# One step of a token mixer: side pieces ahead of the additions of landed rows, or behind them

## The chip, the cores and the metric

The kernel runs on one core of a Trainium2 chip. A core has five engines with instruction queues of their own: TensorE (PE in the profile, its weight loads PEld), VectorE (DVE), ScalarE (ACT), GpSimd (POOL) and SyncE (SP), which here issues nearly all DMAs. The metric is the device time of one execution in microseconds (us); less is better.

## The reference, cut to what matters

One transformer layer on 256 tokens of width 2048, all in float32: a first SwiGLU block, a token mixer, a second SwiGLU block. Ahead of each block the input is normalised, scaled and shifted by rows that a vector `c` yields through one large matrix `w_ada` (2048 x 18432); its nine parts are shift, scale and gate of the three blocks.

```python
ada = (jax.nn.silu(c) @ w_ada + b_ada)[:, None, :]
sh1, sc1, g1, sh2, sc2, g2, sh3, sc3, g3 = jnp.split(ada, N_ADA, axis=-1)
h = _swiglu(_modulate(x, sh1, sc1), ffn1_w_in, ffn1_w_out)
x = _layernorm(ALPHA * x + 0.5 * (1 + g1) * h, ln1_g, ln1_b)
h = _token_mixer(_modulate(x, sh2, sc2), w_in, ...)   # 8 softmax heads with forget gates, 4 mLSTM heads
x = _layernorm(ALPHA * x + (1 + g2) * h, ln2_g, ln2_b)
h = _swiglu(_modulate(x, sh3, sc3), ffn2_w_in, ffn2_w_out)
x = _layernorm(ALPHA * x + 0.5 * (1 + g3) * h, ln3_g, ln3_b)
```

## The kernel before, in words

**Large products.** Each float32 factor is split into a rounded part `hi` and a rest `lo`, and a product is three matmuls (`mm3`, L391 to L393). Weights come in loads of 1 MB (`load_w`, DMA issued by SP at L374) into three buffers `raw`; ACT casts them to `hi` (L145), DVE subtracts to get `lo` (L146), 1024 columns at a time, into six buffers of each kind.

**The ada rows.** `silu(c) @ w_ada` has one row on the left, so it isn't run on PE: for each of 16 blocks of 128 rows, a piece of 512 KB of `w_ada` (tile `ar`, three buffers under the tag `araw`, issued by SP at L168) is scaled by a column of `silu(c)` and added to a tile `acc` on DVE (`ada_acc`, L158 for the first piece, L160 for the others). When 16 pieces are in, a few small steps ("columns") end the group: for a gate, ACT and DVE split `acc` into two tiles that also take `araw` buffers, PE sums over the partitions into two PSUM tiles `bc` (L180), and DVE adds them to `gate` (L217); for a pair of shift and scale, PE transposes (`at`, L193) and DVE reduces (L196). This work is spread over the whole kernel by `pump(n)`: it first adds what was issued in an earlier call (`add_landed`), then runs one small step of a group that is ending (`end_columns`), then issues new pieces, some `n` per call and never more than two that have not been added.

**The mixer.** Its projections run as units of 1 MB of weights, and after each unit `step()` (L991) is called: 4 times in each of four projections of `cols_form_b`, 4 times in each of six of `form_a_pair`, and 12 times in the first two passes of the output projection, 52 in all. `step()` calls `pump(R_MX)` and `advance(NP)`. `advance` takes up to two pieces of the heads' work from the list `side`, each a generator: gates, convolutions, mLSTM heads (`mlstm_head`, `mlstm_out` with its transposes `ytp`, L1244), softmax heads (`fox_head`: logits `lps` on PE, L1078; masks, maxima and reciprocals on DVE, L1083 to L1087; exponentials on ACT, L1086; transposes `ptp`, L1093). The list is empty for the first eight steps; `gates()` is put on it after them. The side pieces issue no DMA. Small PSUM tiles (`aux_tile`: `bc`, `at`, `lps`, `ptp`, `ytp` and so on) share three banks.

**What sets the order.** The program as traced in Python gives each instruction its rank; a planner then fixes each engine's queue from its own estimates of durations: of the instructions that it takes for ready it queues the one of the lowest rank. So rank decides only among ready instructions. One thing binds harder: `ada_acc` calls `tc.keep_in_program_order`, which queues the addition behind the DVE instruction that was traced just ahead of it. On the chip each queue is then fixed, with semaphores where one engine needs another. A DMA that waits for a buffer holds up what stands behind it in SP's queue.

Of the kernel before, what the change touches and what calls it, by code (L numbers as in the profile page):

```python
# [47 lines left out]
def layer_kernel(  # L48
# [178 lines left out]
    def add_landed():  # L227
        while landing:
            ada_acc(*landing.pop(0))

    def end_columns():
        if ada["ends"] and next(ada["ends"], 0) == 0:
            ada["ends"] = None
            ada["done"] += 1

    def next_row():
        if not ada["rows"]:
            if not ada["left"]:
                return ENDED
            ada["rows"] = ada["left"].pop(0)  # L240
        got = next(ada["rows"])
        if got in (None, PAUSE):
            return got
        ada.update(ends=got, rows=None, beside=0)
        next(got)
        return STARTED

    def pump(n):
        add_landed()
        end_columns()  # L250
        ada["owed"] = min(ada["owed"] + n, 3)
        while ada["owed"] >= 1 and len(landing) < 2 and not (ada["ends"] and ada["beside"]):
            got = next_row()
            if got == ENDED:
                break
            if got != STARTED:
                ada["owed"] -= 1
                ada["beside"] += 1
            if got == PAUSE:
                break  # L260
# [427 lines left out]
    NP = 2  # L688
# [288 lines left out]
    def advance(n):  # L977
        for g in list(side):
            if n == 0:
                break  # L980
            got = next(g, 0)
            if got == 0:
                side.remove(g)
            n -= got is not True
# [4 lines left out]
            advance(NP)  # L989

    def step():  # L991
        pump(R_MX)
        advance(NP)

    def wait(names):
        while not done.issuperset(names):
# [3 lines left out]
    def cols_form_b(c0, col, ws, use, name):  # L1000
        ps = {(a, b): mm_tile(f"b_{name}{col}{a}{b}") for b in range(len(ws)) for a in range(2)}
        cb = [sum(ws[:b]) for b in range(len(ws) + 1)]
        copies = emptied[-1:]
        for u in range(4):
            for k4, hi, lo in load_w(W[u * 512:(u + 1) * 512, c0 + col:c0 + col + cb[-1]], 4, cb[-1],
                                     f"{name}{col}_{u}", copies=copies if u else ()):
                k = u * 4 + k4
                for a in range(2):
                    ts_ = slice(a * P, (a + 1) * P)
                    for b in range(len(ws)):  # L1010
                        bs = slice(cb[b], cb[b + 1])
                        mm3(ps[a, b][:, :ws[b]], xhi[:, k, ts_], xlo[:, k, ts_], hi[:, bs], lo[:, bs],
                            k == 0, k == KD - 1)
            step()
        for b in range(len(ws)):
            for a in range(2):
                use(col + cb[b], a, ps[a, b], ws[b])
# [19 lines left out]
    def form_a_pair(ca, cb, name):  # L1037
        ps = [mm_tile(f"pr_{name}{i}") for i in range(2)]
        copies = emptied[-1:]
        cols_form_a(W, ca, [p[:, :T] for p in ps], xT, f"{name}a", step, copies=copies)  # L1040
        cols_form_a(W, cb, [p[:, T:] for p in ps], xT, f"{name}b", step)
        return ps
# [438 lines left out]
```

## Time and profile before

| what | value |
|---|---|
| median of 3 runs | 1930.63 us (1930.4 to 1932.44) |
| the profiled execution, its own time | 1933.45 us |
| its span, first to last instruction | 1931.8 us |
| PE busy / weight loads busy | 97% / 89% of the span |
| DVE busy / ACT busy | 76% / 48% |
| DMA | 510.89 MB, mean 264 GB/s |
| granted TensorE clock | 0.998 of full |

The profile is that of one execution, so sums are made against its 1933.45 us. Busy times are unions of an engine's instructions. A number behind a row's `x` is a count; "[0.77 <-DVE gate L217]" says that the engine sat idle for 0.77 us ahead of that instruction, and what ended it. The stretch in which `side` has work and `step()` is called runs from about 880 to 1130 us.

### The profile page before, as it was taken

To read this page: it belongs to the slowest core of one execution; us is meant where nothing else is said; L and a number is where in the kernel's file an instruction comes from. 1 tells how busy PE (TensorE), PEld (TensorE's weight loads), DVE (VectorE), ACT (ScalarE), POOL (GpSimd) and SP (SyncE) were. 2 spreads that over 40 slices of the span, in tenths; PEclk is the share of its full clock that TensorE was granted. 3 is DMA by queue.
4 is the path that set the end of the run, shared out by engine and by line. 5 is a ranking of instruction groups with operands and counts; after the bars stand their busy time and mean duration, and the time that the engine had idled before them with its cause. 6 is when DMAs were issued, how large, how long until landed. Compare 5 with 4: busy or idle time off the path is not lost.

```text
span 1931.8 us, 32165 instructions
## 1 busy us (share of the span) xinstructions
PE 1882.0 (97%) x13109; PEld 1726.2 (89%) x13109; DVE 1466.0 (76%) x1774; ACT 931.4 (48%) x1296; POOL 54.2 (3%) x85
## 2 busy tenths in 40 slices
PE   3999999999999999999999999999999999999997
PEld 3999999999988888598999776999999999988886
DVE  7889979877778899678787787777775654555776
ACT  3554354444354464745664544555444444444562
POOL 1211100000000000000000000000000000000000
PEclk9999999999999999999999999999999999999999
DMA  9988969989799887489778784998777656655552
GB/s 354 356 312 304 332 209 315 327 297 335 267 336 315 274 302 259 154 311 318 266 252 288 282 296 147 324 313 270 236 260 257 226 196 197 228 189 193 196 195 89
DMA packets 295819, 510.89 MB, mean 264 GB/s; under 512 B 10834, under 2 KB 158962, under 8 KB 294648
## 3 DMA queue, kind: packets, MB, share of 16 engines
q1 hardware_dynamic: 287896, 480.53, 73.2%
q0 software_dynamic: 7776, 28.32, 4.2%
q8 instruction: 102, 1.67, 0.4%
q14 instruction: 45, 0.37, 0.1%
HBM read 506.71 MB, written 2.10 MB: 263 GB/s over the span
## 4 chain that ended last, share of the span: by engine, by line
PE 90%; DVE 5%; DMA 3%; ACT 1%; issue 1%; POOL 0%; SPq 0%; DVEq 0%; ACTq 0%; POOLq 0%
PE gu_f L391 8%; PE gu_f L393 8%; PE gu_f L392 8%; PE o_f L391 8%; PE o_f L393 8%; PE o_f L392 8%; PE s L391 4%; PE s L392 4%; PE s L393 4%; PE pr_f L393 2%; PE pr_f L392 2%; PE pr_f L391 2%; PE fh L393 2%; PE fh L392 2%; PE fh L391 2%; PE fs L392 1%
## 5 line engine op out<-in xcount | busy, mean ns | idle before, releaser
L160 DVE SCALAR_TENSOR_TENSOR acc<-ar,csil,acc 128x1024 f32<-128x1024 f32 x240 | 306.9, 1279 | 33.0 <-DMA ar<-in_w_ada_dram 32.6
L391 PE MATMUL s<-xhi_f,hi_s 128*128 128x256 f32 x768 | 213.3, 279 | 1.7 <-ACT xhi_f L325 0.9
L392 PE MATMUL s<-xlo_f,hi_s 128*128 128x256 f32 x768 | 213.0, 278 | 0.1
L393 PE MATMUL s<-xhi_f,lo_s 128*128 128x256 f32 x768 | 212.4, 277 | 0.0
L393 PE MATMUL gu_f<-xhi_f,lo_f2i 128*128 128x256 f32 x768 | 212.0, 276 | 0.0
L392 PE MATMUL gu_f<-xlo_f,hi_f2i 128*128 128x256 f32 x768 | 212.0, 276 | 0.0
L391 PE MATMUL gu_f<-xhi_f,hi_f2i 128*128 128x256 f32 x768 | 212.0, 276 | 0.0
L146 DVE TENSOR_TENSOR lo_f2i<-raw_f2i,hi_f2i 128x1024 fp32r<-128x1024 f32 x96 | 117.6, 1225 | 100.1 <-ACT hi_f2i L145 100.0
L391 PE MATMUL gu_f<-xhi_f,hi_f1i 128*128 128x256 f32 x640 | 176.8, 276 | 0.0
L393 PE MATMUL gu_f<-xhi_f,lo_f1i 128*128 128x256 f32 x640 | 176.7, 276 | 0.0
L392 PE MATMUL gu_f<-xlo_f,hi_f1i 128*128 128x256 f32 x640 | 176.7, 276 | 0.0
L145 ACT CAST hi_f2i<-raw_f2i 128x1024 fp32r<-128x1024 f32 x96 | 100.8, 1050 | 137.5 <-PE gu_f L392 125.5
L145 ACT CAST hi_s<-raw_s 128x1024 fp32r<-128x1024 f32 x96 | 100.2, 1053 | 114.0 <-PE s L392 86.8
L391 PEld LDWEIGHTS s<-xhi_f,hi_s 128*128 128x128 f32 x768 | 144.8, 189 | 2.0 <-ACT xhi_f L325 1.1
L392 PEld LDWEIGHTS s<-xlo_f,hi_s 128*128 128x128 f32 x768 | 145.0, 189 | 0.4 <-DVE xlo_f L327 0.3
L393 PEld LDWEIGHTS s<-xhi_f,lo_s 128*128 128x128 f32 x768 | 144.6, 189 | 0.3 <-DVE lo_s L146 0.3
L392 PEld LDWEIGHTS gu_f<-xlo_f,hi_f2i 128*128 128x128 f32 x768 | 144.2, 188 | 0.1
L391 PEld LDWEIGHTS gu_f<-xhi_f,hi_f2i 128*128 128x128 f32 x768 | 144.2, 188 | 0.1
L393 PEld LDWEIGHTS gu_f<-xhi_f,lo_f2i 128*128 128x128 f32 x768 | 144.2, 188 | 0.0
L145 ACT CAST hi_f1i<-raw_f1i 128x1024 fp32r<-128x1024 f32 x80 | 83.6, 1050 | 114.6 <-PE gu_f L392 80.3
L146 DVE TENSOR_TENSOR lo_f2o<-raw_f2o,hi_f2o 128x1024 fp32r<-128x1024 f32 x86 | 105.3, 1224 | 43.2 <-ACT hi_f2o L145 43.1
L145 ACT CAST hh<-hT 128x512 fp32r<-128x512 f32 x126 | 77.3, 620 | 114.1 <-PE o_f L392 113.8
(490 smaller groups left out, 5406.9 us busy)
## 6 DMA issues: line engine op xcount, KB each, us to landing
ar<-in_w_ada_dram SPq DMA_DIRECT2D x240, 512.0 KB, 5.9
raw_s<-in_ffn_w_in_dram SPq DMA_DIRECT2D x48, 1024.0 KB, 7.3
raw_f2i<-in_ffn_w_in_dram SPq DMA_DIRECT2D x48, 1024.0 KB, 5.1
raw_f1o<-in_ffn_w_out_dram SPq DMA_DIRECT2D x44, 1024.0 KB, 7.8
raw_f2o<-in_ffn_w_out_dram SPq DMA_DIRECT2D x44, 1024.0 KB, 5.1
raw_f1i<-in_ffn_w_in_dram SPq DMA_DIRECT2D x40, 1024.0 KB, 7.7
ar<-in_w_ada_dram POOLq DMA_DIRECT2D x48, 512.0 KB, 6.9
raw_mxo<-in_w_out_dram SPq DMA_DIRECT2D x16, 1024.0 KB, 8.1
```

Source lines behind the costliest of these rows:

```text
L145: S.copy(hi, src)
L146: V.tensor_tensor(out=lo, in0=src, in1=hi.bitcast(F32), op=ALU.subtract)
L160: ins = V.scalar_tensor_tensor(out=acc, in0=raw, scalar=csil[:, k:k + 1], in1=acc, op0=ALU.mult, op1=ALU.add)
L391: PE.matmul(o, ah, bh, start=start, stop=False)
L392: PE.matmul(o, ah, bl, start=False, stop=False)
L393: return PE.matmul(o, al, bh, start=False, stop=stop)
```

## The change

In `step()` the two calls change places. Nothing is added or removed.

```diff
     def step():
+        advance(NP)
         pump(R_MX)
-        advance(NP)
```

Ahead of it, the additions of a step were traced behind the last split of the unit's weights, and the side pieces behind them; after it, the additions, the small ending steps and the new `ar` loads of a step are traced behind the side pieces of that step.

## Rows read from the trace of the kernel before

**Rows 1.** The page's first lines: span; busy us (share) x instructions.

```profile
span 1931.8 us, 32165 instructions
PE 1882.0 (97%) x13109; PEld 1726.2 (89%) x13109; DVE 1466.0 (76%) x1774; ACT 931.4 (48%) x1296; POOL 54.2 (3%) x85
```

**Rows 2.** Waits of PE, whole span: us in total, times, longest.

```profile
PE cp L741 <- DVE gate L160: 14.8, 1, 14.8
...
PE ptp L1093 <- ACT s L1088: 1.4, 2, 1.0
...
PE ytp L1244 <- DVE gate L217: 0.8, 1, 0.8
...
PE o_mx L393 <- DVE ylo L146: 0.2, 1, 0.2
```

**Rows 3.** Stretches: us, busy us of PE, PEld, DVE, ACT, POOL; PEclk, DMA share, GB/s.

```profile
1090.00:1130.00 40.00, 38.91 (x181) 31.80 (x180) 29.51 (x38) 19.81 (x35) 0.00 (x0) 1.00 0.94 330
1130.00:1185.00 55.00, 54.74 (x262) 45.16 (x260) 47.22 (x69) 18.30 (x25) 2.88 (x4) 1.00 0.68 229
```

**Rows 4.** Groups of 880 to 1130 us: count, busy us, mean ns, idle before, releaser.

```profile
L160 DVE SCALAR_TENSOR_TENSOR acc<-ar,csil,acc 128x1024 f32<-128x1024 f32 x48 | 61.3, 1278 | 5.4 <-DMA ar<-in_w_ada_dram 5.3
L146 DVE TENSOR_TENSOR lo_fv<-raw_fv,hi_fv 128x1024 fp32r<-128x1024 f32 x8 | 9.6, 1219 | 1.5 <-ACT hi_fv L145 1.5
```

**Rows 5.** Waits of SP's queue in 880 to 1130 us: total, times, longest.

```profile
SPq L168 <- DVE acc L160: 55.1, 35, 3.5
SPq L168 <- DMA ar<-in_w_ada_dram: 22.5, 12, 4.7
```

**Rows 6.** Timeline near 1017 us, all engines: start, us, instruction, [idle before].

```profile
1016.46 0.41 PE L180 MATMUL bc<-alo,trir 128*128 128x512 f32 x1
...
1016.71 0.60 PE L1244 MATMUL ytp<-ident,og 128*128 128x128 f32 x4
1017.34 1.28 DVE L217 SCALAR_TENSOR_TENSOR gate<-bc,gate 128x512 f32<-128x512 f32 x2
...
1018.08 0.66 PE L1244 MATMUL ytp<-ident,og 128*128 128x128 f32 x4 [0.77 <-DVE gate L217]
...
1019.67 0.48 DVE L1251 SCALAR_TENSOR_TENSOR yl<-ytp,hcol,yh 128x256 fp32r<-128x256 f32 x1
```

**Rows 7.** Timeline near 1084 us, all engines.

```profile
1083.64 0.75 DVE L158 TENSOR_SCALAR acc<-ar,csil 128x1024 f32<-128x1024 f32 x1 [1.77 <-DMA ar<-in_w_ada_dram]
...
1084.24 0.82 PE L1078 MATMUL lps<-qs 128*128 128x128 f32 x4
1084.31 1.22 DVE L146 TENSOR_TENSOR lo_mxo<-raw_mxo,hi_mxo 128x1024 fp32r<-128x1024 f32 x1
...
1085.44 0.73 DVE L1083 SCALAR_TENSOR_TENSOR s<-lps,ccol,mask 128x128 f32<-128x128 f32 x2
```

**Rows 8.** Timeline near 1120 us, all engines.

```profile
1118.85 1.28 DVE L160 SCALAR_TENSOR_TENSOR acc<-ar,csil,acc 128x1024 f32<-128x1024 f32 x1
...
1119.66 0.18 ACT L1086 ACTIVATION_READ_ACCUMULATOR s<-s,nm 128x1 f32 x1
1120.05 0.22 DVE L1087 RECIPROCAL nm<-nm 128x1 f32<-128x1 f32 x2
...
1120.69 0.84 PE L1093 MATMUL ptp<-ident,s 128*128 128x128 f32 x3 [1.01 <-ACT s L1088]
```

**Rows 9.** Timelines of DVE and PE near 1038 and 1065 us.

```profile
1037.16 0.17 DVE L1087 RECIPROCAL nm<-nm 128x1 f32<-128x1 f32 x1 [1.01 <-ACT s L1086]
1038.10 2.58 DVE L146 TENSOR_TENSOR lo_f1a<-raw_f1a,hi_f1a 128x1024 fp32r<-128x1024 f32 x2 [0.77 <-ACT hi_f1a L145]
...
1039.52 0.28 PE L393 MATMUL pr_f<-xhi_mx,lo_f1a 128*128 128x256 f32 x1
...
1064.51 2.36 DVE L146 TENSOR_TENSOR lo_fv<-raw_fv,hi_fv 128x1024 fp32r<-128x1024 f32 x2 [1.51 <-ACT hi_fv L145]
...
1066.04 0.40 PE L392 MATMUL b_fv<-lo_fv,xhi_mx 128*128 128x512 f32 x1
```

## Prediction

> **What bounds the kernel now.** I read the page's busy times first, then the waits of PE, then the stretch of the mixer, then the waits of SP's queue, and last the timelines around each wait of PE in the mixer. PE is busy for 97% of the span, DVE for 76% [rows 1]. So PE is the engine to ask about, and its waits say where time could be won. The longest of them, 14.8 us, lies ahead of the first product of the kernel and has nothing to do with the mixer [rows 2]. Between 880 and 1130 us, where the change can act, PE waits in three ways only: 1.4 us in two waits of the transposes `ptp` for ACT's scaled exponentials, 0.8 us in one wait of `ytp` for the addition to `gate`, and 0.2 us for a split of `yF` [rows 2]. Together that is 2.4 us, or 0.12% of the time. None of PE's waits in the mixer is for a DMA or for a split of weights, although SP's queue stands still for 55.1 us in that stretch because an `ar` buffer is not yet added (35 times, up to 3.5 us) and 22.5 us more because its former load has not landed [rows 5]. So PE has weights ahead of it, and what the mixer loses is little.
>
> What a measurement of this kernel can tell from no change is about 0.2%, or 3.9 us. The waits that the change could remove are smaller than that.
>
> [...]
>
> **The change, part by part.** Nothing is added or removed. Three kinds of work are moved behind the side pieces of the same step: the additions (48 of 1278 ns and three shorter first ones between 880 and 1130 us [rows 4]), the small ending steps of a group, and the issue of the `ar` loads. The side pieces issue no DMA, so the order in which SP meets the weight loads and the `ar` loads stays as it was; what changes is when an `ar` buffer is free. In the first eight steps there is no side piece and nothing changes. When the rows' groups end does not matter for the rest: each has steps to spare ahead of its use, and the number of rows per step is the same.
>
> *The ending step of a gate, at 1017 us.* Before, the two `bc` tiles take two of the three small PSUM tiles first, the first `ytp` the third, and the second `ytp` waits 0.77 us for the addition to `gate` [rows 6]. After, the two `ytp` come first, then the first `bc`; the second `bc` waits for the first `ytp` to be read. That reading is two pairs of one ACT and one DVE instruction, of which one DVE takes 0.48 us [rows 6]: with three of such a size in a row, 1.4 us, less what PE does in between (the second `ytp`, 0.66 us, and a matmul of `bc`, 0.25 us from its start to the next), some 0.5 us. The ends are 0 (the planner puts products there) and 1.8 us (one more DVE instruction of 1.28 us [rows 4] ahead of the reading). I take 0.5, the sum of the nearest rows: 0.5 less 0.8 is -0.3 us.
>
> *The logits at 1084 us.* DVE stands 1.77 us for a row that has not landed, adds it, splits weights, and only at 1085.44 masks the logits, which PE ended at 1084.24 + 0.82 = 1085.06 [rows 7]. With the addition behind, the mask can start at most 0.4 us sooner. One of PE's two waits for `ptp` hangs on it, with 1.4 less 1.0, or 0.4 us [rows 2]. Ends: 0 and -0.4; the split of 1.22 us stays in front unless it too moves up, so I take the middle, -0.2 us.
>
> *The reciprocal at 1120 us.* An addition that starts at 1118.85 ends at 1120.13 by its duration, the exponentials it keeps waiting were done at 1119.66 + 0.18 = 1119.84, and the reciprocals go at 1120.05 [rows 8]. Behind it, they would go some 0.2 us sooner. PE's wait there is 1.01 us [rows 8], and most of it is the chain mask, maximum, exponential itself. Ends: 0 and -1.0; I take -0.2 us.
>
> *Additions that now stand behind a side piece and ahead of a tight split.* Near 1038 us the last reciprocal of two heads goes at 1037.16, the split of `f1a` starts at 1038.10 after a wait for ACT and its first half is done 1.22 us later, at 1039.32; PE uses it at 1039.52, with 0.2 us to spare [rows 9, 4]. Near 1065 us the split of `fv` ends at 1064.51 + 1.22 = 1065.73, and PE uses it at 1066.04, with 0.3 us to spare [rows 9, 4]. An addition that is tied to the last reciprocal falls just ahead of such a split. Before 1038.10 there is an idle time of 0.77 us, so one addition of 1.28 us costs 0.5 us of delay, of which 0.2 is covered: +0.3 us. Before 1064.51 there is 1.51 us of idle, which covers one addition. Ends: 0, when no row is due there, and +4.6 us, when two additions (2.56 us) delay each of the two splits in full: 2.56 - 0.2 + 2.56 - 0.3. I take one at the first place, +0.3 us, since a step issues 1.42 rows on the mean.
>
> *Later `ar` loads.* An addition that goes later frees its buffer later, and SP, which waits for it, holds up the weights behind it. Ends: 0, since even 55.1 us of such waits cost PE nothing now, and +3.5 us, one longest wait passed on in full [rows 5]. I take +0.4 us, near the first end, by the row that shows no wait of PE for weights [rows 2].
>
> *Loads that no longer hold DVE.* DVE stood 5.3 us for rows that had not landed [rows 4]. That mostly goes, as rows have longer to land; what is late next is the split for which ACT's cast is awaited, so I count nothing beyond the three waits above.
>
> The sum: 1933.45 - 0.3 - 0.2 - 0.2 + 0.3 + 0.4 = 1933.45 us for the profiled execution. It stands 2.8 us above the median of the runs, 1930.63, and the change is the same there: 1930.6 us.
>
> **The rivals.**
>
> *The planner's queues hardly change.* Rank decides only among ready instructions, and rows that landed early may already stand where the new order puts them; only the tie of `ada_acc` binds. For it: the addition at 1118.85 already stands amid a head's work [rows 8]. Against it: the tie is to the DVE instruction traced last, which is another one now in each step with a side piece that uses DVE. It gives 1930.6 us too. Chance 0.14.
>
> *DVE's late additions reach PE (slower).* The mechanism is that of the tight splits above, with two additions at both: +4.6 us, 1935.2. It decides from the point at which additions behind a last reciprocal exceed the idle time and the 0.2 and 0.3 us to spare [rows 9]. For it: DVE takes its queue in order, and at 1083.64 an addition has already held up a split and a mask for 1.77 us [rows 7]. Against it: the additions would have to bunch at just these places. Chance 0.19.
>
> *All waits of PE in the mixer go.* 1.4 + 0.8 + 0.2 is 2.4 us: 1928.2. For it: in two of the three chains an addition stands [rows 7, 8]. Against it: the chain of a head through ACT remains. Chance 0.09; a quarter of that goes beyond, to more than 3.9 us.
>
> *PE loses more than its waits show.* If a mere fiftieth of the 11% in which no weights are loaded [rows 1] were idle time that the side pieces cause, 0.02 x 210 = 4.2 us would go: 1926.4. [...] Chance 0.06.
>
> **How the numbers follow.** My forecast, that the moves take place and add up to nothing, has 0.52. Faster by more than 3.9 us: 0.06 and a quarter of 0.09, 0.08 in all. Slower by more than 3.9 us: 0.19. Within: the forecast, the first rival and the rest of the third, 0.73. The range reaches down to 1927.0, just past all waits gone, and up to 1936.5, past the slower rival's 1935.2 with a third of the 3.5 us of SP's longest wait added; some 0.08 is left out on each side, a little more above.
>
> **What would show it right or wrong.** Right: PE's waits between 880 and 1130 us stay between 1 and 4 us in total, `ytp` no longer waits for `gate`, a `bc` waits for a DVE or ACT instruction on `ytp` instead or nothing does, and DVE's waits for rows fall well below 5.3 us. The slower rival: PE waits for a `lo_` split, near 1038 or 1065 us above all, with an addition just ahead of it on DVE. SP's queue waiting on additions for much more than 55.1 us, with PE or ACT waiting for a `raw_` load and PE for the split behind it, would show my term for late loads too small. The prediction is wrong if the start of the second block's first product moves by more than 4 us either way, or if time is won or lost outside of 880 to 1130 us.

## The result

The kernel changed takes 1936.19 us (median of 8 runs, 1934.27 to 1938.6), the kernel before 1931.78 us beside it (8 runs); the ratio is 1.0023, 95% interval 1.0014 to 1.0031. A second set of 11 runs gave 1935.73 against 1932.32 us, ratio 1.0018 (1.0010 to 1.0027). One run of all, at 2104.6 us with a granted clock of 0.852 (`e10`, below), was in a slower state and is left out of every median and ratio. The change costs 3.4 to 4.4 us, where I had forecast none. The time lies inside the range of 1927.0 to 1936.5, but the case that came about is the slower one, to which I gave 0.19.

The profile after, with the lines that answer to those of before. First the page's head [rows 1]:

```profile
span 1933.8 us, 32176 instructions
PE 1883.5 (97%) x13109; PEld 1727.7 (89%) x13109; DVE 1468.0 (76%) x1774; ACT 931.3 (48%) x1296; POOL 55.1 (3%) x85
```

The same work is done in a span 2.0 us longer. What PE waits for, whole span [rows 2]:

```profile
PE bc L180 <- DVE gate L217: 2.2, 1, 2.2
...
PE pr_f L393 <- DVE lo_f0a L146: 0.8, 1, 0.8
...
PE ptp L1093 <- ACT s L1088: 0.5, 1, 0.5
PE o_mx L391 <- ACT yhi L145: 0.4, 1, 0.4
...
PE b_fv L392 <- DVE lo_fv L146: 0.2, 1, 0.2
```

`ytp` no longer waits, and one of the two waits for `ptp` is gone; in their place stand `bc` with 2.2, `lo_f0a` with 0.8, `yhi` with 0.4 and `lo_fv` with 0.2 us. With the 0.2 us for `ylo` that stand there as before, PE waits 4.3 us in the mixer, 2.4 before; the 14.8 us ahead of the kernel's first product are as they were. SP's queue from 880 to 1130 us [rows 5]:

```profile
SPq L168 <- DVE acc L160: 108.4, 38, 12.8
```

Its wait for additions doubles, and the longest goes from 3.5 to 12.8 us. The additions themselves, in the groups of that stretch [rows 4], take as long as before and wait 3.3 us for rows instead of 5.3:

```profile
L160 DVE SCALAR_TENSOR_TENSOR acc<-ar,csil,acc 128x1024 f32<-128x1024 f32 x48 | 61.5, 1280 | 3.6 <-DMA ar<-in_w_ada_dram 3.3
```

**Where the time went.** Spans of single executions differ by some us for reasons that have nothing to do with the mixer, so I cut the trace at PE's first matmul on certain tiles: the first `pr_m` product (about 902 us), the first `pr_f` product on `f0a`, on `f1a` and on `f1b`, the first `o_mx` product, its first on `kept`, and the first of the second block (`ge`). Each number is the time from one such start to the next, in us; the first column is the time ahead of `pr_m`.

```
                        to m0a  m0a-f0a  f0a-f1a  f1a-f1b  f1b-o_mx  o_mx-kept  kept-ge   m0a-ge
before                  902.6   101.88    27.22    14.48     39.37     76.26     23.28    282.49
e1_before_again         901.4   101.88    26.59    14.48     39.37     76.35     23.28    281.95
after                   902.2   101.88    29.78    14.59     40.58     74.76     23.27    284.87
e9_after_again          902.2   101.88    29.88    14.62     40.44     74.75     23.27    284.85
e2_ends_first           901.8   101.88    31.10    14.53     40.71     74.75     23.27    286.26
e3_bc_other_bank        905.5   101.88    27.22    15.95     40.64     74.75     23.27    283.72
e4_gate_end_later       901.0   101.88    26.75    17.79     42.25     75.20     23.77    287.64
e5_loads_last           900.9   101.88    26.89    14.59     39.38     75.72     23.28    281.75
e6_adds_first           900.6   101.88    26.33    14.55     39.37     78.56     23.28    283.98
e7_outproj_only         902.3   101.88    26.53    14.48     39.37     75.09     23.28    280.63
e10_outproj_again       903.3   101.88    27.00    14.50     39.37     75.20     23.27    281.24
e8_proj_only            900.4   101.88    29.95    14.48     40.92     74.75     23.28    285.25
e11_free_additions      900.2   105.36    27.97    16.19     39.38     74.63     23.28    286.81
e12_ar_by_pool          905.3   101.88    29.30    14.60     40.14     74.77     23.28    283.96
```

What is ahead of `pr_m` scatters over 5 us without system, most of it in the first block, from PE's first `s` product to its first `gu_f` product (about 38 to 310 us; it takes 270.2 to 274.1); in two executions of one kernel the rest repeats to 0.15 us, but for the stretch from `f0a` to `f1a`, in which `ytp` waits now and then. Mean against mean of two executions each, the kernel changed loses 2.9 us from `f0a` to `f1a`, 0.1 and 1.1 in the next two stretches, and wins 1.6 us from `o_mx` to `kept`: 2.6 us in all. Up to `o_mx` that is 4.2 us, though PE's waits there (2.2, 0.8, 0.4 and 0.2 us) add up to 3.6: here 0.6 us of the loss do not stand in the idle time that the profile shows.

**From f0a to f1a: two additions among the `og` pieces, and the cast of `ahi`.** DVE's timeline of the kernel changed near 1005 us, then ACT's:

```profile
1004.11 1.28 DVE L160 SCALAR_TENSOR_TENSOR acc<-ar,csil,acc 128x1024 f32<-128x1024 f32 x1
1005.30 0.48 DVE L1238 SCALAR_TENSOR_TENSOR og<-yM,rr,og 128x256 f32<-128x256 f32 x1
1005.70 1.28 DVE L160 SCALAR_TENSOR_TENSOR acc<-ar,csil,acc 128x1024 f32<-128x1024 f32 x1
...
1008.48 1.22 DVE L146 TENSOR_TENSOR alo<-acc,ahi 128x1024 fp32r<-128x1024 f32 x1
1009.61 2.36 DVE L146 TENSOR_TENSOR lo_f0a<-raw_f0a,hi_f0a 128x1024 fp32r<-128x1024 f32 x2
```

```profile
1007.01 1.05 ACT L145 CAST ahi<-acc 128x1024 fp32r<-128x1024 f32 x1 [2.17 <-DVE acc L160]
...
1008.23 2.00 ACT L145 CAST hi_f0a<-raw_f0a 128x1024 fp32r<-128x1024 f32 x2
```

The last two additions of the gate's group stand between the `og` pieces, so ACT, which takes its queue in order, stands 2.17 us at the gate's cast `ahi`, with the weights' cast `hi_f0a` behind it; `lo_f0a` starts at 1009.61, 5.5 us behind the first product on `f0a` (1004.1), and PE waits for it 0.8 us. In the kernel before, DVE runs all eight `og` pieces and then `lo_f0a` at 1007.09, 2.6 us behind that product (1004.5):

```profile
1003.91 3.26 DVE L1238 SCALAR_TENSOR_TENSOR og<-yM,rr,og 128x256 f32<-128x256 f32 x8 [1.77 <-POOL rr L271]
1007.09 2.35 DVE L146 TENSOR_TENSOR lo_f0a<-raw_f0a,hi_f0a 128x1024 fp32r<-128x1024 f32 x2
```

**The second `bc`.** DVE and ACT of the kernel changed, 1017 to 1022 us, against [rows 6]:

```profile
1018.61 1.23 DVE L146 TENSOR_TENSOR lo_f1a<-raw_f1a,hi_f1a 128x1024 fp32r<-128x1024 f32 x1 [0.65 <-ACT hi_f1a L145]
1019.75 1.28 DVE L160 SCALAR_TENSOR_TENSOR acc<-ar,csil,acc 128x1024 f32<-128x1024 f32 x1
1020.95 0.48 DVE L1251 SCALAR_TENSOR_TENSOR yl<-ytp,hcol,yh 128x256 fp32r<-128x256 f32 x1
1021.35 0.68 DVE L217 SCALAR_TENSOR_TENSOR gate<-bc,gate 128x512 f32<-128x512 f32 x1
```

```profile
1017.53 2.00 ACT L145 CAST hi_f1a<-raw_f1a 128x1024 fp32r<-128x1024 f32 x2 [3.51 <-PE ytp L1244]
1019.43 0.83 ACT L1250 ACTIVATE yh<-ytp,hcol 128x256 fp32r<-128x256 f32 x2
```

The second `bc` needs the PSUM tile that the first addition to `gate` empties. Ahead of that addition DVE has a split, an ada addition and a `yl`; the split needs the casts `hi_f1a` on ACT, and the `yl` needs a `yh` that stands behind them. ACT stands 3.51 us ahead of these casts. The profile puts that down to `ytp` in this execution; in the other one of this kernel, `e9`, it puts the same wait down to the load of `raw_f1a`. That load is late: SP issues it at 1012.00 in the kernel changed, as the first two splits of `f0a` are done (1009.61 + 2.36 = 1011.97). ACT in `e9`, then SP in the first execution:

```profile
1017.67 2.00 ACT L145 CAST hi_f1a<-raw_f1a 128x1024 fp32r<-128x1024 f32 x2 [3.50 <-DMA raw_f1a<-in_w_in_dram]
```

```profile
1012.00 0.37 SPq L374 DMA_DIRECT2D raw_f1a<-in_w_in_dram  x1
```

Counted from the first product on `f0a`, the load goes at 7.9 us, in the kernel before at 5.0. So by the trace the delay of `lo_f0a` is paid for twice: at once, with 0.8 us, and through the next weights, at `bc`.

**The split of `fv`, and the reciprocal.** DVE near 1065 us [rows 9] and near 1120 us [rows 8], then PE at the second place:

```profile
1065.10 0.16 DVE L1087 RECIPROCAL nm<-nm 128x1 f32<-128x1 f32 x1 [0.33 <-ACT s L1086]
1065.18 2.59 DVE L160 SCALAR_TENSOR_TENSOR acc<-ar,csil,acc 128x1024 f32<-128x1024 f32 x2
1067.68 1.22 DVE L146 TENSOR_TENSOR lo_fv<-raw_fv,hi_fv 128x1024 fp32r<-128x1024 f32 x1
...
1120.24 0.22 DVE L1087 RECIPROCAL nm<-nm 128x1 f32<-128x1 f32 x2
1120.37 1.27 DVE L160 SCALAR_TENSOR_TENSOR acc<-ar,csil,acc 128x1024 f32<-128x1024 f32 x1
```

```profile
1122.70 0.82 PE L1093 MATMUL ptp<-ident,s 128*128 128x128 f32 x6
```

Two additions right behind the last reciprocal hold up the split, as the slower rival had it, but PE waits only 0.2 us for it. Counted from the first product on `f1b` (1048.43 and, before, 1046.16), the last reciprocal goes at 16.67 us in both kernels, and the split 0.9 us later than before (19.25 against 18.35): the idle time of 1.51 us that DVE had there [rows 9] takes up most of the 2.59 us. At 1120 us the addition now stands behind the reciprocals, and `ptp` waits for nothing.

**The first `yhi` of the output projection.** ACT of the kernel changed:

```profile
1086.43 1.05 ACT L145 CAST hi_mxo<-raw_mxo 128x1024 fp32r<-128x1024 f32 x1 [0.56 <-DMA raw_mxo<-in_w_out_dram]
1087.38 1.06 ACT L1049 COPY yF<-b_fv 128x512 f32<-128x512 f32 x2
1088.33 1.15 ACT L145 CAST yhi<-yF 128x512 fp32r<-128x512 f32 x2
```

Here a weight load is late: ACT stands for `raw_mxo`, and `yF` and `yhi`, for which PE waits 0.4 us, stand behind that cast. What holds the load is a buffer that DVE empties late, and not an `ar` load ahead of it in SP's queue. The first of these loads and the split ahead of it:

```profile
1070.01 1.22 DVE L146 TENSOR_TENSOR lo_fv<-raw_fv,hi_fv 128x1024 fp32r<-128x1024 f32 x1
```

```profile
1071.26 0.38 SPq L374 DMA_DIRECT2D raw_mxo<-in_w_out_dram  x1
```

The split ends at 1071.23; SP had been through with its last `ar` load at 1070.45. The next two loads, at 1074.72 and 1079.39, also go 0.02 us behind the end of a split of `fv`. On DVE six additions stand between the last reciprocal and the last of these splits, three in the kernel before; counted from the first product on `f1b`, the three loads go 2.1 us later than before.

### The profile page after: what moved, and what is told of

It is laid out like the page before. It is cut to its first block, busy times and chain, and to the rows that moved or that the text cites. A ratio compares the mean times of both kernels' runs of the same rounds, so it can differ in the third digit from the quotient of the medians.

```text
span 1933.8 us, 32176 instructions
## 1 busy us (share of the span) xinstructions
PE 1883.5 (97%) x13109; PEld 1727.7 (89%) x13109; DVE 1468.0 (76%) x1774; ACT 931.3 (48%) x1296; POOL 55.1 (3%) x85
## 4 chain that ended last, share of the span: by engine, by line
PE 78%; issue 12%; DVE 5%; DMA 3%; ACT 2%; POOL 1%; DVEq 0%; SPq 0%; POOLq 0%; ACTq 0%
PE gu_f L392 8%; PE gu_f L393 8%; PE gu_f L391 8%; PE o_f L391 8%; PE o_f L393 8%; PE o_f L392 8%; PE s L392 3%; PE s L391 3%; PE s L393 3%; PE fh L393 2%; PE fh L392 2%; PE fh L391 1%; PE fs L391 1%; PE fs L392 1%; PE fs L393 1%
## 5 line engine op out<-in xcount | busy, mean ns | idle before, releaser
L160 DVE SCALAR_TENSOR_TENSOR acc<-ar,csil,acc 128x1024 f32<-128x1024 f32 x240 | 307.6, 1282 | 31.4 <-DMA ar<-in_w_ada_dram 30.4
```

The source lines that it names most:

```text
L160: ins = V.scalar_tensor_tensor(out=acc, in0=raw, scalar=csil[:, k:k + 1], in1=acc, op0=ALU.mult, op1=ALU.add)
```

## The experiments

A step has four parts: A the additions of landed rows, E the ending step of a group, R the issue of new rows, S the side pieces. The kernel before runs A E R S, the kernel changed S A E R. The theory at the start: late additions and late ends delay, on queues of fixed order, what feeds PE at several places. Rivals: the later `ar` loads hold weights up on SP's queue; one PSUM wait for `bc` alone; chance from run to run.

**e1_before_again**, the kernel before, unchanged.

> The kernel before, unchanged, against itself: ratio 1.000, and its spans and its waits of PE give the spread against which the trace of one execution of the changed kernel (span 2.0 us longer) and the median of eight runs (4.4 us longer) are to be read. If the queues alone decide, PE's waits between 880 and 1130 us are the same three as in the first trace: ptp 1.4, ytp 0.8, o_mx 0.2 us. If the runs differ mostly by chance (a rival), they come out elsewhere.

Measured: 1931.77 us against 1931.53, ratio 0.9998 (0.9989 to 1.0006). In this execution `ytp` does not wait; the 0.77 us of [rows 6] come and go, so the 0.8 us that I had booked as won there can be won in some executions only.

**e2_ends_first**, order E S A R.

```diff
     def step():
+        end_columns()
         advance(NP)
-        pump(R_MX)
+        add_landed()
+        more_rows(R_MX)     # the rest of pump
```

> The changed kernel with the small ending steps of a group put back ahead of the side pieces (order in a step: ending step, side pieces, additions, new loads). My theory, that the time is lost where the bc tiles queue behind the ytp tiles for a PSUM bank and where additions stand late in DVE's and ACT's queues: PE's wait of 2.2 us before bc goes, the 0.8 us before lo_f0a and the 0.4 to 0.5 us near 1068 and 1088 us stay: some 1.5 to 2.2 us less than the changed kernel, so 1934 to 1934.7 against 1936.2. The rival, that late ar loads hold up SP's queue and so the weights (108 us of waits for additions there against 55): nothing changes in time, since additions and loads stay where the change put them, 1936.2.

Measured: 1936.6 us, ratio 1.0021 (1.0013 to 1.0030): a miss. PE's waits, 950 to 1150 us:

```profile
PE ytp L1249 <- DVE gate L217: 2.1, 1, 2.1
```

With the ends first the two `bc` go ahead, and the second `ytp` waits for the additions to `gate` just as long. The wait changed its name, not its size. No addition of an `ar` row stands just ahead of them here; at 1019.28 they follow the split of `f1a`, which waits for a cast that stands 3.59 us for the load of `raw_f1a`:

```profile
1018.14 1.23 DVE L146 TENSOR_TENSOR lo_f1a<-raw_f1a,hi_f1a 128x1024 fp32r<-128x1024 f32 x1 [0.72 <-ACT hi_f1a L145]
```

What is late is DVE, and through it the weights.

**e3_bc_other_bank**, the kernel changed with `bc` of this gate in another PSUM pool.

```diff
-            bc = aux_tile(f"bc{tag}_{i}")
+            bc = (mm_tile if tag == "5_0" else aux_tile)(f"bc{tag}_{i}")
```

> The changed kernel with the two bc tiles of the first gate in the mixer taken from the five larger PSUM banks and not from the three small ones; nothing else. My theory: both bc follow the two ytp at once, PE's wait of 2.2 us before bc is gone, and the time falls by 2.2 us to about 1934.0. Rival (late loads): the wait goes, but the time does not, as PE meets it again at the next weights.

Measured: 1934.95 us, ratio 1.0014 (1.0005 to 1.0023). `bc` waits no more, but the next head's logits `lps` do. PE's waits, and DVE's timeline ahead of that wait:

```profile
PE lps L1075 <- DVE yl L1251: 1.3, 1, 1.3
```

```profile
1034.53 1.28 DVE L160 SCALAR_TENSOR_TENSOR acc<-ar,csil,acc 128x1024 f32<-128x1024 f32 x1 [1.93 <-DMA ar<-in_w_ada_dram]
```

An addition again, one for whose row DVE first stands 1.93 us, with `yl`, whose PSUM tile the logits want, behind it. The bank was not the cause alone: by the table 1.2 us of the 2.2 are won (283.72 against 284.87).

**e4_gate_end_later**, the kernel changed with this gate's split two steps later and its `bc` one step less far behind.

```diff
     def ada_sum(acc, tag):
+        if tag == "5_0":
+            for _ in range(2):
+                yield
         ...
-        for _ in range(2):
+        for _ in range(1 if tag == "5_0" else 2):
             yield
         ...
-            for _ in range(2):             # in ada_gate
+            for _ in range(3 if tag == "5_0" else 2):
                 yield next(bcs)
```

> The changed kernel with the ending of the first gate in the mixer two steps (its cast and split) and one step (its bc) later, so that ACT does not stand at that cast for the late addition ahead of the weights' cast, and bc meets no ytp. My theory: the 2.2 us before bc and the 0.8 us before lo_f0a both go, 3 us in all: about 1933.2. If the cast on ACT has no part in it: 2.2 us, 1934.0. If the late loads do it: no change, 1936.2.

Measured: 1937.77 us, ratio 1.0031 (1.0021 to 1.0041). PE's waits:

```profile
PE lps L1078 <- DVE yl L1254: 3.0, 1, 3.0
PE o_mx L394 <- ACT yhi L145: 2.1, 1, 2.1
PE pr_f L396 <- DVE lo_f0a L146: 0.3, 1, 0.3
```

The wait for `lo_f0a` falls to 0.3 us. `hi_f0a` now goes ahead of `ahi`, and `lo_f0a` starts 5.1 us behind the first product on `f0a`, 0.5 us sooner than in the kernel changed and still 2.4 us later than before: so `ahi` on ACT accounts for some 0.5 us of the delay, and what is left is about the two additions (2.56 us) that still stand ahead of `lo_f0a` on DVE. The other waits move on and grow. Treating the places one by one does not help as long as the additions stay behind.

**e5_loads_last**, order A E S R: the new rows alone are issued behind the side pieces.

```diff
     def step():
-        pump(R_MX)
+        add_landed()
+        end_columns()
         advance(NP)
+        more_rows(R_MX)
```

> Additions and ends stand ahead of the side pieces as in the kernel before; the issue of new rows alone stands behind them, as in the kernel changed. Theory (late additions and late ends cost PE the time, later loads cost nothing): the time of before, ratio 1.000 +- 0.0007, some 1931.5 us; PE's waits between 950 and 1130 us as before, ptp and ytp, 2 to 2.5 us in all, none for bc, lo_f0a or yhi; SP's queue waits for additions some 55 us. Rival (the later ar loads hold up the weights behind them on SP's queue): the time of the kernel changed, ratio 1.002, some 1936 us, with SP waiting for additions for about 108 us.

Measured: 1931.64 against 1932.23 us, ratio 0.9994 (0.9986 to 1.0003). SP's queue from 880 to 1130 us:

```profile
SPq L168 <- DVE acc L160: 55.2, 35, 3.5
```

Issuing later costs nothing, as long as the additions are early. e2 differs from this kernel only in where the additions are, and takes 4.5 us longer by the table.

**e6_adds_first**, order A S E R; `add_landed()` alone goes first.

> Only the additions stand ahead of the side pieces; the ends and the new rows stand behind them. Theory that the additions carry the loss: 0.7 to 1.2 us above before, from a wait of bc for the gate of 0.7 to 1.2 us (the 2.2 us of the kernel changed less one addition of 1.28 us), and no wait for lo_f0a or lo_fv; ratio 1.0005, some 1932.3 us. Rival that the ends carry it: the wait of bc stays at 2.2 us and the time is 2 to 4 us above before, ratio 1.001 to 1.002.

Measured: 1933.88 us, ratio 1.0009 (1.0000 to 1.0018). From `f0a` to `o_mx` it is as short as before (80.25 us, by the table, against 81.07 and 80.44; the kernel changed has 84.95). DVE's timeline at the gate:

```profile
1016.13 0.48 DVE L1256 SCALAR_TENSOR_TENSOR yl<-ytp,hcol,yh 128x256 fp32r<-128x256 f32 x1
1016.53 0.68 DVE L217 SCALAR_TENSOR_TENSOR gate<-bc,gate 128x512 f32<-128x512 f32 x1
...
1019.03 1.28 DVE L160 SCALAR_TENSOR_TENSOR acc<-ar,csil,acc 128x1024 f32<-128x1024 f32 x1
```

The ends are as late as in the kernel changed, but no addition stands among them. Neither `bc` of this gate nor `lo_f0a` waits, and the load of `raw_f1a` goes 4.4 us behind the first product on `f0a` (before 5.0, changed 7.9): in the projections the additions carry the loss. What is over comes later, from the ending step of another gate, which now meets the output projection. PE's waits, 950 to 1150 us:

```profile
PE bc L180 <- ACT yF L1110: 1.4, 1, 1.4
```

Expected were 0.7 to 1.2 us of a wait for `gate`; the total came out near that by another wait.

**e7_outproj_only** and **e10_outproj_again**, one kernel twice: the new order in the 12 steps of the output projection, that of before in the other steps.

```diff
+    def late_step():
+        advance(NP)
+        pump(R_MX)
...
-    out_proj(w_out[0], y_rows, KD, "mx", step, finish2, before, 4, 3, spare2)
+    out_proj(w_out[0], y_rows, KD, "mx", late_step, finish2, before, 4, 3, spare2)
```

> The new order stands in the 12 steps of the out projection alone; the steps of the projections keep the order of before. Theory (the loss of the changed kernel arises up to 1085 us, and 1.5 us of it are won back at 1120 us, where the addition no longer stands ahead of the reciprocal): 0.5 to 1.5 us below before, ratio 0.9993 to 0.9998, some 1930.6 us, with the waits of ytp and ptp before 1118 us as before and no wait of ptp near 1120 us. Rival (the gain at 1120 us comes only because PE got there 3.5 us later): no change, ratio 1.000, with the wait near 1120 us still at 1 us. Rival (late loads cost): slower.

> The order of before in the projections, the new order in the 12 steps of the out projection, once more. Theory: 280.6 us in the stretch from pr_m to ge as in its first run, 1.3 to 1.9 us less than before, ratio 0.9990 to 0.9993. Rival (its -1.0 us was chance): ratio 1.000.

Measured: 1931.26 us, ratio 0.9992 (0.9984 to 1.0001), and 1932.58 us (10 runs), ratio 1.0002 (0.9993 to 1.0011). The stretch is 1.0 to 1.6 us shorter than that of before. DVE of the first run:

```profile
1117.46 0.22 DVE L1091 RECIPROCAL nm<-nm 128x1 f32<-128x1 f32 x2
1117.59 1.27 DVE L160 SCALAR_TENSOR_TENSOR acc<-ar,csil,acc 128x1024 f32<-128x1024 f32 x1
```

Counted from the first `o_mx` product, the reciprocals go at 1117.46 - 1084.61 = 32.9 us, in the kernel before at 1120.05 - 1085.54 = 34.5 [rows 8]: 1.7 us sooner, and the wait of `ptp` there goes. So this part of the change wins something over 1 us in the trace; the medians can't confirm it, and I don't call this kernel faster.

**e8_proj_only**, the converse: the new order in the projections, the order of before in those 12 steps.

> The new order stands in the steps of the projections alone; the 12 steps of the out projection keep the order of before. Theory: the whole loss up to 1085 us, 3.5 us, and nothing won back at 1120 us: 1935 to 1938 us, ratio 1.0017 to 1.003. Rival (the wait at 1120 us goes because PE is late there, whatever the order): the time of the kernel changed, 1936 us, without a wait of ptp near 1120 us.

Measured: 1934.3 us, ratio 1.0010 (1.0001 to 1.0018). "Nothing won back" is a miss: the last stretch of the output projection takes 74.75 us here too. DVE and PE near 1120 us:

```profile
1118.85 1.27 DVE L160 SCALAR_TENSOR_TENSOR acc<-ar,csil,acc 128x1024 f32<-128x1024 f32 x1
1120.05 0.21 DVE L1091 RECIPROCAL nm<-nm 128x1 f32<-128x1 f32 x2
```

```profile
1121.26 0.82 PE L1097 MATMUL ptp<-ident,s 128*128 128x128 f32 x6
```

The addition stands ahead of the reciprocals, as before, and yet `ptp` waits for nothing: PE comes late enough. Up to `o_mx` this kernel has lost 4.6 us. So the 1.6 us that the kernel changed wins back, which has lost 4.2 by then, need no new order in these 12 steps.

**e9_after_again**, the kernel changed.

> The kernel changed, once more, to size its loss. From the first product of pr_m to the first of ge (PE starts in the trace) it takes 284.9 us against 282.0 and 282.5 in two executions of the kernel before. Theory (that stretch holds the whole loss): 2.4 to 2.9 us above before in the medians, ratio 1.0012 to 1.0015. Rival (more is lost than this stretch shows): 4.4 us again, ratio 1.0023.

Measured: 1935.73 against 1932.32 us, ratio 1.0018, between the two expectations.

**e11_free_additions**, the kernel changed, with the additions made in `step()` not tied to the program order.

```diff
-        tc.keep_in_program_order(ins)
+        if not ada["free"]:        # True inside pump(R_MX) of step()
+            tc.keep_in_program_order(ins)
```

> The kernel changed, but an addition made in a step of the mixer is not tied to the program order, so that the planner may put it ahead of side pieces that are traced before it. Theory (the tie behind the side pieces is what makes the additions late): the waits for lo_f0a and bc or ytp go, SP's waits for additions fall back to some 55 us, and the time is that with additions traced first, 281.5 to 284 us from pr_m to ge, ratio 0.9995 to 1.001. Rival (the planner takes instructions in the order of the trace where several are ready, tie or not): 284.9 us, ratio 1.002, with the same waits.

Measured: 1938.19 us (5 runs), ratio 1.0035 (1.0021 to 1.0048). Neither was right. SP's waits for additions and PE's waits:

```profile
SPq L169 <- DVE acc L160: 57.1, 34, 4.3
```

```profile
PE nps L1211 <- DVE dm L1206: 1.8, 1, 1.8
PE bc L181 <- DVE gate L218: 1.6, 1, 1.6
PE lps L1078 <- DVE yl L1254: 1.4, 1, 1.4
```

The tie does make SP wait twice as long: 57.1 us without it. But the loss is larger, and in new places. DVE near 981 us:

```profile
981.24 1.28 DVE L160 SCALAR_TENSOR_TENSOR acc<-ar,csil,acc 128x1024 f32<-128x1024 f32 x1 [0.84 <-DMA ar<-in_w_ada_dram]
982.44 0.48 DVE L1205 TENSOR_TENSOR dm<-dm,trir 128x128 f32<-128x128 f32 x2
```

DVE stands 0.84 us for a row, adds it for 1.28, and only then does `dm`, for which PE waits. ACT was done with `dm` at 979.43. As I read these rows, it is not being late that costs, but standing just ahead of an instruction that PE needs next. ACT's 2.17 us at `ahi` are of the same kind.

**e12_ar_by_pool**, the kernel changed, with the `ar` loads from the projection `f1` to `fv` issued on POOL's queue, so that no weight load stands behind them.

```diff
-            SP.dma_start(raw..., src[k * P:(k + 1) * P])
+            (G_ if ada["pool"] else SP).dma_start(raw..., src[k * P:(k + 1) * P])
```

> The kernel changed, but the ar loads issued from the last pair of projections (f1) to the end of the last projection (fv) go through POOL's queue, which is idle there, so that the weight loads raw_mxo on SP's queue don't stand behind an ar load that waits for its addition. In the kernel changed SP waits 12.8 us so, ACT then waits 3.95, 1.82 and 0.56 us for raw_mxo, and yF and yhi stand behind those casts. Theory (late additions also work through late weight loads there): ACT's waits for raw_mxo fall below 2.5 us in all, PE's wait for yhi of 0.4 us goes, and the stretch from f1b to o_mx falls from 40.5 to between 39.9 and 40.2 us (the wait for lo_fv stays); the stretch up to f1b as in the kernel changed; in all some 0.4 us less than it, less or more by what is then won back at 1120 us. Rival (yhi waits because of the order on ACT alone, the loads are hidden): 40.5 us and the wait for yhi stay.

Measured: 1935.71 against 1932.82 us, ratio 1.0014 (1.0005 to 1.0023). The wait for `yhi` goes and the stretch from `f1b` to `o_mx` takes 40.14 us instead of 40.5, as the theory had it; but ACT's waits for `raw_mxo` fall only from 6.3 to 6.0 us (4.36, 0.82 and 0.77), not below 2.5. SP's queue now waits for the buffers themselves: 24.3 us, up to 14.9, for splits of `fv`, which stand behind additions on DVE. Counted from the first product on `f1b`, the first two loads of `raw_mxo` are issued at 22.8 and 26.3 us in both kernels, and the third, on which `yhi` hangs, at 31.4 instead of 31.0. So the `ar` loads in SP's queue held up none of them, and its 12.8 us were hidden.

The third load's cast starts 6.2 us behind its issue here, 7.0 and 6.9 us in the two executions of the kernel changed, and that is where the 0.3 to 0.4 us come from. Whether moving the `ar` loads did it is not shown: for the first load these two executions differ by 1.4 us (8.8 and 7.4).

**What this settles.** The medians against before follow the stretch from `pr_m` to `ge`. The differences by the table, from the mean of before's two executions, and those of the medians are +2.7 and +4.4 (changed), +2.6 and +3.4 (again), +4.0 and +5.1 (e2), +1.5 and +3.4 (e3), +5.4 and +6.2 (e4), -0.5 and -0.6 (e5), +1.8 and +1.7 (e6), -1.6 and -1.0, -1.0 and +0.3 (e7, e10), +3.0 and +2.1 (e8), +4.6 and +5.9 (e11), +1.7 and +2.9 us (e12). So the mixer holds the bulk of the loss. Of the 0.8 to 1.8 us by which the kernel changed lies above its stretch, 0.3 to 0.4 lie outside the span from first to last instruction: a run's time less its span is 2.0 to 2.1 us there (medians of 8 and 11 runs), 1.7 in the kernel before; why is not shown. The rest stays open; the scatter ahead of `pr_m` is larger than that.

## Why the prediction was wrong

- **The gate at 1017 us: the term that was off by most.** I put the wait of `bc` at 0.5 us, from three DVE instructions of 0.48 us, and gave 1.8 as the end, with one addition ahead. It measured 2.2. The prediction took the queues of a good case: the two casts of 2.00 us on ACT and the split of 1.23 us on DVE ahead of `yh` and `yl`, all late by the load of `raw_f1a`, were not in the sum. That the end of 1.8 comes near is luck: in e2 no addition stands just ahead of the gate's, and the wait is 2.1. On the other side, the 0.77 us to be won were there in one execution of before and not in the other.
- **Two additions at 1005 us and the cast `ahi`: the step that failed first.** I looked for late additions at 1038 and 1065 us only, and wrote that when the rows' groups end does not matter. Both failed at `lo_f0a`: two additions stand ahead of it on DVE, and the split of a gate's sum, whose input is the later of them, stands on ACT amid the weights' casts. `lo_f0a` came 2.9 us later, of which e4 gives some 0.5 to `ahi`. That cost 0.8 us at once, in e9 0.9, and made the load of `raw_f1a` late, to which the wait of `bc` goes back.
- **Tight splits.** The mechanism was right at 1065 us, where two additions (2.59 us) stand between the last reciprocal and the split; the size was not: 0.2 us of wait, not 2.3 (2.56 less 0.3). That price left out the idle time of 1.51 us that the same paragraph names; with it, it is 2.56 - 1.51 - 0.3 = 0.75 us, and the place near 1038 us comes to 2.56 - 0.77 - 0.2 = 1.6 instead of 2.4. At 1038 us nothing happened.
- **Logits and reciprocal.** At 1084 us nothing was won: `ptp` waits 0.5 us where [rows 2] leaves 0.4. At 1120 us the wait went whole, 1.0 us (the stretch is 1.6 us shorter), where I had -0.2; e8 shows that PE's lateness alone would have done it.
- **Later loads.** The size came out, +0.4 us at `yhi`, but by luck: the weights that were late there waited for splits behind additions on DVE, and no `ar` load in SP's queue held them up. Further on one did: at 1095.19 us an `ar` load goes that had waited 6.4 us for its addition, and the load of `raw_mxo` behind it follows at 1095.66 without a wait of its own; no wait of PE hangs on it. The sign that I had named came too, 108.4 us of SP's waits with ACT waiting for `raw_mxo`; but e11, with 57.1 us, loses more, and e5 shows that issuing later costs nothing, so the sign says little.
- **The rival that came nearest.** "Late additions reach PE" gave 1935.2 us; measured were 1935.7 to 1936.2. Its mechanism is the cause, but its two places were the wrong ones: one cost 0.2 us and one nothing, and most of the loss came through `lo_f0a` and `gate`. That 1935.2 is so near is luck, since the price of 4.6 us left out the idle times; with them it is 2.3. By its own argument against it, that the additions would have to bunch, 0.19 was too low: the tie puts each addition behind whatever a side piece does last, and at `lo_f0a`, `lo_fv` and `yl` PE's next input stood right behind.
- **The share of weight loads.** The rival by which PE loses more than its waits show, 1926.4 us, took a fiftieth of the 11% of the span without weight loads (some 210 of 1931.8 us) for idle time. No run shows these 210 us to be idle time of PE: in [rows 3] PEld is busy for 82% of a stretch in which PE is busy for 54.74 of 55.00 us, and the 1.1 us in which PE is idle from 1090 to 1130 us are about its wait of 1.01 us for `ptp` [rows 8]. PEld's share stayed at 89% while the time moved by 3.4 to 4.4 us, and PE's waits in the mixer went from 2.4 to 4.3 us. The rival did not come about.

## What to carry to other kernels

When background work is moved on an engine that runs its queue in order, list for each place the instruction that falls in behind it and who waits for that one, the slow engine's casts for the background work's own ending included (ACT stood 2.17 us at `ahi`); a sum of waits that go is only half of it. Follow the delay on to the next load too: a late split frees its buffer late, and the load that needs the buffer comes late (`raw_f1a`, 2.9 us). How long SP's queue waits in all said little (108.4 us in the kernel changed, 57.1 in e11, which loses more); look at what the issue of the late load follows. The wait that moved from tile to tile with the order (`bc` 2.2 us, `ytp` 2.1, `lps` 1.3) pointed to DVE, which releases these tiles, and not to the number of tiles alone. And compare stretches between the same two matmuls: here most repeat to 0.15 us, where the way to the mixer scatters by 5.

## What the runs showed that I had not expected

The scatter from run to run sits almost wholly ahead of the mixer: 900.2 to 905.5 us to the first `pr_m` in 14 executions, though no edit touches a step before 880 us (the 71 us ahead of `pr_m`, from the mixer's first product on, agree to 0.15 us), while the 101.88 us behind it agree to the last digit in all but e11, which changes them. A kernel that had lost 4.6 us by `o_mx` (e8) got 1.6 of them back without any edit there, since a wait further on (`ptp`, 1.0 us) was for something that did not depend on PE's being on time.
